# A hybrid decoder block with a product-key expert layer: expert-row fetches tied to TensorE's progress, and a second buffer in a lookup

## The chip, the cores and the metric

The kernel runs on one core of one Trainium2 chip. The metric is device time in microseconds of one execution, lower is better. Three timed executions of the kernel before are known, and one execution that was also profiled. Engines are called as the profile calls them: PE is TensorE (PEld its weight loads), DVE is VectorE, ACT is ScalarE, POOL is GpSimd, SP is SyncE, which here only issues DMAs.

## What is computed

One decoder layer over 512 tokens of width 1024: adaLN modulation, an input projection, sliding-window attention beside a short convolution, an output projection, and then an expert layer (PEER) over 16384 single-neuron experts. Only the expert layer matters for the change. Cut to it, the reference is:

```
q = (xt @ wq).reshape(T, 8 heads, 2, 128)
sc = einsum('thpd,hpkd->thpk', q, subkeys)          # 128 keys per half
vals, ids = top_k(sc, 16)
cand = vals[:, :, 0, :, None] + vals[:, :, 1, None, :]
top, pos = top_k(cand, 16)                          # 16 experts per head, 128 per token
idx = take(ids0 * 128 + ids1, pos); g = softmax(top)
a   = u_tab[idx] . x                                # one number per token and expert
out = sum over experts of g * gelu(a) * v_tab[idx]
x  += gate2 * out
```

## The kernel before

The 512 tokens are treated in two ways. For the first 384 (three chunks of 128) the expert layer is computed **densely**: all 16384 experts are taken as 128 groups of 128, and for each group j TensorE multiplies the tokens by the u table (the "u product" of j, line 197 to 199, called from `first`) and the gated result by the v table (the "v product" of j, line 958 to 960, called from `second`); a token's unused experts have a gate of zero. For the last 128 tokens the 128 chosen experts per token are **gathered**: `fetch` (line 764) has POOL issue an indirect DMA that brings, for expert number k of each of the 128 tokens, one row of 1024 numbers into a tile of 128 x 1024 (512 KB). There are 128 such fetches from the u table, each followed by a dot product on DVE (`dot`, line 774), then 128 from the v table, each followed by a multiply-and-add on DVE into the tile `ga` (line 872). Another 64 u fetches, earlier, serve the last 64 of the dense tokens (`last_dense`).

A u or v product takes three matmuls per block, since each operand is split into a high and a low part: a 512 KB table tile `raw` is loaded by SP (line 178, five buffers), ACT writes its high part `hi` (line 173), DVE the low part `lo` (line 174). A u product is 24 matmuls of 320 columns, a v product 18 matmuls of 512 columns.

The program, by stages in time, ends with two that the change touches:

- The **lookup** of the dense tokens (`lookup`, six steps of three chunks and two halves). Each step expands a table of key numbers on ACT into the tile `ex` (line 665), compares on DVE, multiplies the comparison by `ex` (line 686) and sums. Four u products are called between two steps (`LOOK`), so ACT's copies `sp<-pa` and `hi` stand between the expansions in ACT's queue. `ex` has one buffer for the three-chunk lookup (line 661).
- The **dense stage** (line 1005 on): a loop over j, 0 to 127. It calls the v product of j; from j = 64 on it also calls the u product of j + 8 (`first`), so u products end with j = 119. Each j needs its v tile (and its u tile), and every eighth j loads a block `G` of the gates (1536 KB); before j = 64 each pair of j also loads 320 KB `sp`. Beside each v product the loop runs a number of steps of `gathered()`, the generator that does the fetches: `PACE` (line 45) is the allowance per j, 1.75 before j = 64 and 4.2 from there on, and a fetch with its arithmetic takes 1.3 of it.

A fetch takes its tile in turn from two pools, `row` (six buffers, shared with `ga`) and `row2` (four buffers; the profile and the order write both as `row`). What stands in the queues is settled at build time: a scheduler goes over the whole program, orders the instructions of each engine by its own estimates and by which buffers are free, and adds the semaphore waits. On the chip each engine, POOL and SP too, runs its queue strictly in that order, so an instruction that waits holds all behind it.

Of the kernel before, what the change touches and what calls it, by code (L numbers as in the profile page):

```python
# [9 lines left out]
F16 = mybir.dt.float16  # L10
# [8 lines left out]
P = 128  # L19
# [11 lines left out]
NJ = 128  # L31
# [10 lines left out]
LAST = 8  # L42
NR = 3
WHEN = (-1, 0, 2, 3)
PACE = (1.75, 4.2)

# [40 lines left out]
def body(tc, p):  # L89
    nc = tc.nc  # L90
# [18 lines left out]
    def bank(name):  # L109
        return psm.tile([P, 512], F32, tag="m", name=name)  # L110
# [55 lines left out]
    def after(ins, mark):  # L166

        if mark is not None:
            tc.add_manual_dep(ins.ins, mark.ins.name, mybir.DependencyInfo(
                mybir.DependencyClass.Sync, mybir.DependencyReason.DATA), reason="pace")  # L170
# [10 lines left out]
    def parts(src):  # L181

        raw = load(src)
        h = hl.tile([P, D], F32R, tag="h", bufs=4, name="hi")
        l = hl.tile([P, D], F32R, tag="l", bufs=4, name="lo")
        split(h, l, raw)
        return h, l

    def weights_of(src):

        h, l = parts(src.rearrange("p a b -> p (a b)"))
        return (lambda k: h[:, k * P:(k + 1) * P]), (lambda k: l[:, k * P:(k + 1) * P])

    def mm3(ps, w, rh, rl, ks=range(DC), k0=0, k1=DC - 1):
        wh, wl = w
        for k in ks:
            nc.tensor.matmul(ps, wh(k), rh(k), start=(k == k0), stop=False)  # L197
            nc.tensor.matmul(ps, wh(k), rl(k), start=False, stop=False)  # L198
            mark[0] = nc.tensor.matmul(ps, wl(k), rh(k), start=False, stop=(k == k1))  # L199
# [13 lines left out]
    def tmp(name):  # L213
        return tp.tile([P, T], F32, name=name, **T2)
# [65 lines left out]
    for m, k in enumerate(ORDER):  # L280
# [10 lines left out]
        f = tmp("f")  # L291
# [184 lines left out]
    for step in PLAN.split():  # L476
        n = [int(x) for x in step[1:]]
# [104 lines left out]
    for r, (dst, cs) in enumerate(((hN, slice(TU - HT, TD)), (h2N, slice(TD, T)))):  # L582
        pg = [bank("pg0"), bank("pg1")]
        for k in range(DC):
            b = mod[:, 24 + k:25 + k]
            f = fs[k]
# [19 lines left out]
    def first():  # L606
        j = lead[0]
        if j == NJ:
            return
        lead[0] += 1  # L610
        w = weights_of(p["uL"][j])
        ps = psa.tile([P, TU], F32, tag="a", name="pa")
        mm3(ps, w, lambda k: h2H[:, k, :], lambda k: h2L[:, k, :])
        m, i = divmod(j, 2)
        if i == 0:
            ring[m] = up.tile([P, 2, TU], F32, name="sp", bufs=3) if j < SPILL else \
                rg.tile([P, 2, TU], F32, name="ge", bufs=RING)
        nc.scalar.activation(ring[m][:, i], ps, AF.Gelu_apprx_tanh)  # L618
        if i and j < SPILL:
            nc.sync.dma_start(Ad[m], ring.pop(m))  # L620
# [30 lines left out]
    def lookup(n, R, hs=slice(0, 8)):  # L651

        pl, pos = R["pool"], R["pos"][:, :, hs]
        nh = hs.stop - hs.start

        def it(name, dt, tag):
            return pl.tile([P, n, nh, 16], dt, tag=f"{tag}{n}", name=name, bufs=1)

        def wide(name):
            return rt.tile([P, nh, 16, 16], F16, name=name, **R2) if n == 1 else \  # L660
                pl.tile([P, nh, 16, 16], F16, tag=f"{name}{n}", name=name, bufs=1)

        def expanded(c, q):
            x = wide("ex")
            nc.scalar.activation(x, R["I"][:, c, hs, q, :, None].to_broadcast([P, nh, 16, 16]), AF.Copy)
            return x

        p4, p2 = it("p4", U32, "da"), it("p2", U32, "db")
        nc.vector.tensor_single_scalar(p4, pos, 4, op=OP.logical_shift_right)
        nc.vector.tensor_single_scalar(p2, pos, 2, op=OP.logical_shift_right)  # L670
        a, b = it("ra", F16, "ra"), it("rb", F16, "rb")
        nc.vector.scalar_tensor_tensor(a, p2, -12.0, p4, op0=OP.add, op1=OP.max)
        l12, b1 = it("l12", U32, "da"), it("rb1", F32, "db")
        nc.vector.tensor_single_scalar(l12, pos, 12, op=OP.bitwise_and)
        nc.vector.scalar_tensor_tensor(b1, pos, 64.0, l12, op0=OP.is_lt, op1=OP.mult)
        l2 = it("l2", U32, "da")
        nc.vector.tensor_single_scalar(l2, pos, 3, op=OP.bitwise_and)
        nc.vector.tensor_add(b, b1, l2)
        sh = [P, nh, 16, 16]
        for c in reversed(range(n)):  # L680
            for q, r, dst in ((0, a, R["i"]), (1, b, R["j"])):
                x = expanded(c, q)
                eq = wide("eq")
                nc.vector.tensor_tensor(eq, iotaA[:, None, :, :].to_broadcast(sh),
                                        r[:, c, :, None, :].to_broadcast(sh), op=OP.is_equal)
                nc.vector.tensor_mul(eq, eq, x)
                w = 8
                while w > 1:
                    nc.vector.tensor_add(eq[:, :, 0:w, :], eq[:, :, 0:w, :], eq[:, :, w:2 * w, :])
                    w //= 2  # L690
                nc.vector.tensor_add(dst[:, c, hs], eq[:, :, 0, :], eq[:, :, 1, :])
                yield
# [52 lines left out]
    last = None  # L745
    for hp in range(16):
# [3 lines left out]
        last = now  # L750
    scores(15, *last)
    weights(ND, Rd)
    first()
    first()
    more = [False, []]

    def numbers(dst, R, c, ks=slice(0, P)):
# [6 lines left out]
    def fetch(tab, e):  # L764
        more[0] = bool(more[1]) and not more[0]
        t = more[1][0].tile([P, D], F32, name="row2", bufs=4) if more[0] else r4.tile([P, D], F32, name="row", **R4)
        nc.gpsimd.indirect_dma_start(out=t, out_offset=None, in_=tab,  # L767
                                     in_offset=bass.IndirectOffsetOnAxis(ap=e, axis=0))
        return t

    def dot(a, e, h):
        t = fetch(p["uR"], e)
        junk = rt.tile([P, D], BF16, name="junk", **R2)
        nc.vector.scalar_tensor_tensor(junk, t, 1.0, h, op0=OP.mult, op1=OP.mult, accum_out=a)  # L774
# [39 lines left out]
    for c in range(ND):  # L814
# [3 lines left out]
        cs = slice(c * P, (c + 1) * P)  # L818
# [7 lines left out]
        n = P if c < ND - 1 else P - HT  # L826
# [19 lines left out]
    def gathered():  # L846

        Rg = results(1, rg)
        ei = rg.tile([P, P], I32, name="eG")
        av = rg.tile([P, P], F32, name="av")  # L850
        yield from route(Rg, ei, range(0, 4))
        others = route(Rg, ei, range(4, 8))
        for k in range(P):
            dot(av[:, k:k + 1], ei[:, k:k + 1], h2N)
            yield 1.3
            if k < P // 2:
                yield next(others, 0.0)
            if k == P // 2 - 1:
                for _ in others:
                    yield 2.0  # L860
                weights(1, Rg)
                yield 1.0
        nc.scalar.activation(av, av, AF.Gelu_apprx_tanh)
        nc.vector.tensor_mul(av, av, Rg["g"].rearrange("p c a b -> p (c a b)"))
        ga = r4.tile([P, D], F32, name="ga", **R4)
        vR = p["vL"].rearrange("j i d -> (j i) d")
        for k in range(P):
            t = fetch(vR, ei[:, k:k + 1])
            if k == 0:
                nc.vector.tensor_scalar_mul(ga, t, av[:, 0:1])  # L870
            else:
                nc.vector.scalar_tensor_tensor(ga, t, av[:, k:k + 1], ga, op0=OP.mult, op1=OP.add)  # L872
            yield 1.3
        total[0] = ga
# [72 lines left out]
    def second(js, ws):  # L947

        ops = [(*w, *parts(p["vL"][j])) for j, w in zip(js, ws)]
        for c, hf in [(c, hf) for hf in range(2) for c in range(ND)] if len(js) == 1 else \  # L950
                [(c, hf) for c in range(ND) for hf in range(2)]:
            cs = slice(c * P, (c + 1) * P)
            hs = slice(hf * 512, hf * 512 + 512)
            for j, (wh, wl, vh, vl) in zip(js, ops):
                if j == 0:
                    acc[c, hf] = bank(f"o{c}{hf}")
                o = acc[c, hf]
                nc.tensor.matmul(o, wh[:, cs], vh[:, hs], start=(j == 0), stop=False)  # L958
                nc.tensor.matmul(o, wh[:, cs], vl[:, hs], start=False, stop=False)  # L959
                nc.tensor.matmul(o, wl[:, cs], vh[:, hs], start=False, stop=(j == NJ - 1))  # L960

    def load_x1(c):
        x1 = r4.tile([P, D], F32, name="x1", **R4)
# [41 lines left out]
    for j in range(0, NJ, 2):  # L1005
        ws = gated(j // 2)
        for i in range(2):
            if j >= SPILL:
                first()
            if j < NJ - 2:  # L1010
                second([j + i], ws[i:])
            todo += PACE[j >= SPILL]
            while todo > 0:
# [75 lines left out]
```

## Time and profile before

| | |
|---|---|
| timed executions | 1494.27, 1496.88, 1503.24 us (median 1496.88) |
| the profiled execution, its own time | 1503.74 us |
| its span, first to last instruction | 1502.0 us |
| mean granted TensorE clock, share of full speed | 0.981 |
| busy share of the span: PE, DVE, ACT, POOL | 95%, 85%, 41%, 32% |
| moved by DMA | 432.07 MB |

The profile gives for each engine its instructions with start, duration and what they waited for, and for DMA the bytes and the mean busy share of 16 DMA engines. PE's busy time is a union of pipelined matmuls, so that PE seems busy where it is not at its peak; how fast it really goes is read from the starts of its matmuls. "Share" of DMA can go a little over 1, since a packet that starts in a window is counted there in full.

### The profile page before, as it was taken

The page shows a single profiled execution, that of the slowest core. Times are in us where ns is not written, and L with a number is a line of the kernel's source. Part 1 is how long each engine was busy: PE and PEld are TensorE (multiplying, and loading weights), DVE is VectorE, ACT ScalarE, POOL GpSimd, SP SyncE. Part 2 cuts the span into 40 slices and gives each one's busy share as a digit, 9 for nine tenths or more (in the row PEclk, how much of TensorE's full clock was granted, in tenths as well). Part 3 has the DMA queues.
Part 4 walks back from the last instruction along what each step waited for, and adds up shares of the span by engine and source line. Part 5 has one row for each costly group of instructions (what it writes and reads, how often), then busy time and mean ns, then how long its engine had stood idle before and what let it go on. Part 6 is the DMA issues. An engine that isn't in the chain of part 4 may idle for free.

```text
span 1502.0 us, 21357 instructions
## 1 busy us (share of the span) xinstructions
PE 1424.6 (95%) x7696; PEld 1239.3 (83%) x7696; DVE 1269.5 (85%) x2330; ACT 616.5 (41%) x1029; POOL 478.4 (32%) x324
## 2 busy tenths in 40 slices
PE   6999998999978999999999989999989999999998
PEld 4777776888977999999888867778879888889986
DVE  7878886999897899968799989899989999996445
ACT  4534537334543444454434333333424334244341
POOL 0000000000144133300234756667667677750000
PEclk9999999999988999999999999999999999999999
DMA  8644544332698699967899999999999999996443
GB/s 286 222 165 144 182 156 143 96 94 83 214 321 322 243 368 368 376 243 267 321 402 363 406 402 405 390 402 377 380 402 369 403 387 405 401 390 213 141 126 126
DMA packets 138283, 432.07 MB, mean 288 GB/s; under 512 B 13121, under 2 KB 39873, under 8 KB 136641
## 3 DMA queue, kind: packets, MB, share of 16 engines
q1 hardware_dynamic: 92096, 262.92, 48.2%
q0 software_dynamic: 46080, 167.79, 29.4%
q8 instruction: 60, 0.98, 0.3%
q14 instruction: 47, 0.38, 0.1%
HBM read 390.78 MB, written 39.85 MB: 287 GB/s over the span
## 4 chain that ended last, share of the span: by engine, by line
DMA 16%; DVE 13%; PE 13%; issue 10%; POOL 1%; ACT 1%; DVEq 0%; POOLq 0%; ACTq 0%; SPq 0%
DMA raw<-in_vL 6%; DMA raw<-in_uL 5%; DVE ga L872 4%; DMA row<-in_uR,eG 3%; DVE lo L174 3%; DVE junk L774 3%; PE o L959 3%; PE o L960 2%; PE o L958 2%; PE pa L197 2%; PE pa L199 2%; PE pa L198 2%; DVE wwl L174 2%; POOL row L767 1%; DVE w L941 1%
## 5 line engine op out<-in xcount | busy, mean ns | idle before, releaser
L173 ACT ACTIVATE hi<-raw 128x1024 fp32r<-128x1024 f32 x298 | 312.8, 1056 | 435.1 <-PE pa L198 137.9
L174 DVE TENSOR_TENSOR lo<-raw,hi 128x1024 fp32r<-128x1024 f32 x298 | 363.6, 1222 | 116.3 <-ACT hi L173 113.8
L197 PE MATMUL pa<-h2H,hi 128*128 128x320 f32 x1024 | 322.5, 315 | 24.8 <-ACT sp L618 19.6
L199 PE MATMUL pa<-h2H,lo 128*128 128x320 f32 x1024 | 320.2, 313 | 1.1 <-DVE lo L174 1.1
L198 PE MATMUL pa<-h2L,hi 128*128 128x320 f32 x1024 | 320.2, 313 | 0.0
L960 PE MATMUL o<-hi,wwl 128*128 128x512 f32 x768 | 303.3, 395 | 7.0 <-DVE wwl L174 4.0
L959 PE MATMUL o<-lo,wwh 128*128 128x512 f32 x768 | 303.5, 395 | 5.7 <-DVE lo L174 4.8
L958 PE MATMUL o<-hi,wwh 128*128 128x512 f32 x768 | 302.9, 394 | 5.9 <-ACT hi L173 5.9
L767 POOL DMA_INDIRECT row<-in_uR,eG x128 | 201.0, 1570 | 218.1 <-DVE w L941 96.2
L767 POOL DMA_INDIRECT row<-in_uR,eH x64 | 80.2, 1253 | 559.9 <-DVE lo L174 400.0
L767 POOL DMA_INDIRECT row<-in_vL,eG x128 | 197.0, 1539 | 88.6 <-DVE ga L872 56.9
L197 PEld LDWEIGHTS pa<-h2H,hi 128*128 128x128 f32 x1024 | 195.8, 191 | 29.5 <-ACT sp L618 21.0
L198 PEld LDWEIGHTS pa<-h2L,hi 128*128 128x128 f32 x1024 | 195.5, 191 | 2.1
L199 PEld LDWEIGHTS pa<-h2H,lo 128*128 128x128 f32 x1024 | 195.3, 191 | 1.9 <-DVE lo L174 1.9
L960 PEld LDWEIGHTS o<-hi,wwl 128*128 128x128 f32 x768 | 145.7, 190 | 44.7 <-DVE wwl L174 11.3
L959 PEld LDWEIGHTS o<-lo,wwh 128*128 128x128 f32 x768 | 145.5, 189 | 39.2 <-DVE lo L174 9.1
L958 PEld LDWEIGHTS o<-hi,wwh 128*128 128x128 f32 x768 | 145.7, 190 | 35.5 <-ACT hi L173 7.0
L872 DVE SCALAR_TENSOR_TENSOR ga<-row,av,ga 128x1024 f32<-128x1024 f32 x127 | 163.9, 1290 | 2.8 <-DMA row<-in_vL,eG 0.5
L774 DVE SCALAR_TENSOR_TENSOR junk<-row,h2N 128x1024 bf16<-128x1024 f32 x128 | 152.8, 1222 | 8.2 <-DMA row<-in_uR,eG 7.6
L940 ACT ACTIVATE w<-G 128x64 f32<-128x64 f32 x128 | 25.8, 248 | 240.0 <-DVE wwl L174 228.0
L916 PE MATMUL gps<-B,A 128*128 128x128 f16 x384 | 90.9, 297 | 1.9 <-DVE B L908 1.9
L774 DVE SCALAR_TENSOR_TENSOR junk<-row,hN 128x1024 bf16<-128x1024 f32 x64 | 78.1, 1221 | 15.2 <-DMA row<-in_uR,eH 15.2
(263 smaller groups left out, 1939.4 us busy)
## 6 DMA issues: line engine op xcount, KB each, us to landing
raw<-in_uL SPq DMA_DIRECT2D x128, 512.0 KB
raw<-in_vL SPq DMA_DIRECT2D x128, 512.0 KB
Gd<-st SPq DMA_DIRECT2D x12, 2048.0 KB
G<-Gd SPq DMA_DIRECT2D x16, 1536.0 KB
ada<-in_ada SPq DMA_DIRECT2D x32, 512.0 KB
Ad<-sp SPq DMA_DIRECT2D x32, 320.0 KB
sp<-Ad SPq DMA_DIRECT2D x32, 320.0 KB
raw<-in_w_in SPq DMA_DIRECT2D x18, 512.0 KB
```

Of the source, the lines that this page charges most:

```text
L173: nc.scalar.activation(h, f, AF.Copy)
L174: nc.vector.tensor_sub(l, f, h.bitcast(F32))
L197: nc.tensor.matmul(ps, wh(k), rh(k), start=(k == k0), stop=False)
L198: nc.tensor.matmul(ps, wh(k), rl(k), start=False, stop=False)
L199: mark[0] = nc.tensor.matmul(ps, wl(k), rh(k), start=False, stop=(k == k1))
L767: nc.gpsimd.indirect_dma_start(out=t, out_offset=None, in_=tab, in_offset=bass.IndirectOffsetOnAxis(ap=e, axis=0))
L774: nc.vector.scalar_tensor_tensor(junk, t, 1.0, h, op0=OP.mult, op1=OP.mult, accum_out=a)
L872: nc.vector.scalar_tensor_tensor(ga, t, av[:, k:k + 1], ga, op0=OP.mult, op1=OP.add)
L916: nc.tensor.matmul(o, A[:, b, :, t], B1[:, b, :, t], start=True, stop=False)
L958: nc.tensor.matmul(o, wh[:, cs], vh[:, hs], start=(j == 0), stop=False)
L959: nc.tensor.matmul(o, wh[:, cs], vl[:, hs], start=False, stop=False)
L960: nc.tensor.matmul(o, wl[:, cs], vh[:, hs], start=False, stop=(j == NJ - 1))
```

## The change

Three edits. `PACE` goes from 1.75 and 4.2 to 1.85 and 4.4. The three-chunk lookup gets two buffers for `ex`. And `fetch` ties its DMA to a v product: each call of `second` puts the last matmul of its v product on a list that keeps two; the next fetch, if two are there, takes the older one off and waits for it. So the first fetch that is called after the v product of j waits until TensorE has ended that of j - 1, and the fetches called after it, up to the next v product, wait for nothing new.

```diff
-PACE = (1.75, 4.2)
+PACE = (1.85, 4.4)
...
-                pl.tile([P, nh, 16, 16], F16, tag=f"{name}{n}", name=name, bufs=1)
+                pl.tile([P, nh, 16, 16], F16, tag=f"{name}{n}", name=name, bufs=2 if name == "ex" else 1)
...
+    done = []
     more = [False, []]
...
-        nc.gpsimd.indirect_dma_start(out=t, out_offset=None, in_=tab,
-                                     in_offset=bass.IndirectOffsetOnAxis(ap=e, axis=0))
+        d = nc.gpsimd.indirect_dma_start(out=t, out_offset=None, in_=tab,
+                                         in_offset=bass.IndirectOffsetOnAxis(ap=e, axis=0))
+        if len(done) > 1:
+            after(d, done.pop(0))
         return t
...
-                nc.tensor.matmul(o, wl[:, cs], vh[:, hs], start=False, stop=(j == NJ - 1))
+                last = nc.tensor.matmul(o, wl[:, cs], vh[:, hs], start=False, stop=(j == NJ - 1))
+        done.append(last)
+        del done[:-2]
```

`after(ins, mark)` adds a dependency: `ins` waits for `mark`. No instruction is added or taken away on PE, DVE or ACT, and PE's order is the same. DVE, POOL, ACT and SP get another order, since the scheduler knows of the new waits.

**POOL, dense stage, about the u rows 105 to 115 of the 128, before and then after.** `row_10469` and the like are tiles of the pool `row2`, plain `row` of the other; `in_uR` is the u table by rows, `eG` the expert numbers; `DMASW` are earlier fetches, `DVE` the release of a buffer, `PE` the new wait.

```order
L767 DMA row_10469<-in_uR,eG 128x1024 [waits DMASW0_49,DVE_49]
L767 DMA row<-in_uR,eG 128x1024 [waits DMASW1_49,DVE_49]
L767 DMA row_10542<-in_uR,eG 128x1024 [waits DMASW2_49,DVE_49]
L767 DMA row<-in_uR,eG 128x1024 [waits DMASW3_49,DVE_49]
L767 DMA row_10550<-in_uR,eG 128x1024 [waits DMASW4_49,DVE_49]
L767 DMA row<-in_uR,eG 128x1024 [waits DMASW5_49,DVE_49]
```

```order
L768 DMA row_10421<-in_uR,eG 128x1024 [waits DMASW1_49,DVE_49,PE_49]
L768 DMA row_10429<-in_uR,eG 128x1024 [waits DMASW2_49,DVE_49]
L768 DMA row_10493<-in_uR,eG 128x1024 [waits DMASW3_49,DVE_49]
L768 DMA row_10501<-in_uR,eG 128x1024 [waits DMASW4_49,DVE_49]
L768 DMA row_10574<-in_uR,eG 128x1024 [waits DMASW5_49,DMASW1_49,DVE_49]
L768 DMA row<-in_uR,eG 128x1024 [waits DMASW6_49,PE_49]
L768 DMA row<-in_uR,eG 128x1024 [waits DMASW7_49]
L768 DMA row<-in_uR,eG 128x1024 [waits DMASW0_49,PE_49]
L768 DMA row<-in_uR,eG 128x1024
```

Before, a fetch waited only for its buffer and an earlier fetch. Now about one in three or four also waits for PE, and those behind it in the queue wait with it. The PE wait of `row_10421` is for the v product of j = 73, the next two for 74 and 75.

**DVE, the end of the gathering, before and then after.** `lo<-raw,hi` is one table tile's low part (u or v), `ga<-row` uses one fetched v row, `w` and `wwl` prepare the gates of two j.

```order
L872 SCALAR_TENSOR_TENSOR ga<-row,av,ga 128x1024
L174 TENSOR_TENSOR lo<-raw,hi 128x1024
L941 TENSOR_TENSOR w<-ge,G 128x2x320
L872 SCALAR_TENSOR_TENSOR ga<-row_13710,av,ga 128x1024
L872 SCALAR_TENSOR_TENSOR ga<-row,av,ga 128x1024
L174 TENSOR_TENSOR lo<-raw,hi 128x1024
L872 SCALAR_TENSOR_TENSOR ga<-row_13716,av,ga 128x1024
L872 SCALAR_TENSOR_TENSOR ga<-row,av,ga 128x1024
L174 TENSOR_TENSOR lo<-raw,hi 128x1024
L174 TENSOR_TENSOR wwl<-w,wwh 128x768
L174 TENSOR_TENSOR lo<-raw,hi 128x1024
```

```order
L875 SCALAR_TENSOR_TENSOR ga<-row_13493,av,ga 128x1024
L875 SCALAR_TENSOR_TENSOR ga<-row,av,ga 128x1024
L174 TENSOR_TENSOR wwl<-w,wwh 128x768
L875 SCALAR_TENSOR_TENSOR ga<-row_13499,av,ga 128x1024
L174 TENSOR_TENSOR lo<-raw,hi 128x1024
L875 SCALAR_TENSOR_TENSOR ga<-row,av,ga 128x1024
L174 TENSOR_TENSOR lo<-raw,hi 128x1024
L875 SCALAR_TENSOR_TENSOR ga<-row_13570,av,ga 128x1024
L153 TENSOR_TENSOR dg<-cst,mod 128x1024
L875 SCALAR_TENSOR_TENSOR ga<-row,av,ga 128x1024
L174 TENSOR_TENSOR lo<-raw,hi 128x1024
```

Before, the last row is used behind the v tile of j = 106 and 34 more `lo` follow it. Now it is used behind the v tile of j = 120 and 7 follow. Counted over DVE's whole order, the rows used from behind the `lo` of one stage's first v tile to that of the next are, for j = 0 to 22, 23 to 63, 64 to 104, 105 to 118 and 119 on: 23, 79, 149, 5, 0 before; 12, 55, 138, 48, 3 after.

**ACT, the start of the lookup, the difference.** `ex` is the expansion, `sp<-pa` the copy of a u product out of PSUM, `hi` a table tile's high part, `Rg` a softmax.

```order
 L665 ACTIVATE ex<-I_2116 128x2048
 L618 ACTIVATE sp<-pa 128x320
-L173 ACTIVATE hi<-raw 128x1024 x2
-L618 ACTIVATE sp<-pa 128x320
-L173 ACTIVATE hi<-raw 128x1024
+L173 ACTIVATE hi<-raw 128x1024
+L665 ACTIVATE ex<-I_2116 128x2048
+L618 ACTIVATE sp<-pa 128x320
+L173 ACTIVATE hi<-raw 128x1024 x2
 L699 ACT_TABLE_LOAD
 L699 ACTIVATE Rg_2114<-Rg_2114 128x384
```

The second `ex` has moved up. From there on each `ex` stands where the one before it stood: the third at the old second's place, and the sixth at the old fifth's, while the old sixth's place is empty. DVE's order in the lookup is the same but for one `lo` that stands two rows later.

## Rows read from the trace of the kernel before

**Rows 1.** Page, DMA in 40 equal slices of 37.55 us: busy tenths, GB/s

```profile
DMA  8644544332698699967899999999999999996443
GB/s 286 222 165 144 182 156 143 96 94 83 214 321 322 243 368 368 376 243 267 321 402 363 406 402 405 390 402 377 380 402 369 403 387 405 401 390 213 141 126 126
```

**Rows 2.** Windows, dense stage in five: length, engines busy (x), clock, DMA share, GB/s

```profile
core 0: us, PE busy (x) PEld busy (x) DVE busy (x) ACT busy (x) POOL busy (x), PEclk, DMA share, GB/s
...
730.95:831.09 100.14, 96.69 (x417) 78.53 (x415) 92.66 (x216) 39.60 (x62) 46.30 (x34) 0.98 0.99 372
831.09:1022.49 191.40, 180.70 (x763) 143.67 (x761) 169.02 (x242) 62.39 (x101) 128.57 (x79) 0.97 1.03 401
1022.49:1351.87 329.38, 318.59 (x1723) 283.70 (x1723) 310.72 (x301) 122.11 (x189) 223.15 (x144) 0.99 1.01 390
1351.87:1458.55 106.68, 106.68 (x591) 96.53 (x589) 56.54 (x52) 43.26 (x66) 0.00 (x0) 1.00 0.50 159
1458.55:1502.00 43.45, 38.64 (x168) 30.98 (x166) 21.45 (x26) 10.27 (x14) 0.00 (x0) 1.00 0.37 133
```

**Rows 3.** Windows of line 958 alone, six matmuls per v product: PE, PEld (x)

```profile
730.95:831.09 100.14, 54.37 (x139) 26.35 (x139) 0.98 0.99 372
831.09:1022.49 191.40, 97.95 (x246) 47.09 (x245) 0.97 1.03 401
1022.49:1351.87 329.38, 96.32 (x247) 46.31 (x247) 0.99 1.01 390
```

**Rows 4.** Timeline of PE, 757.9 to 762.5 us: line 958, seventh start after the first

```profile
758.26 0.39 PE L958 MATMUL o<-hi,wwh 128*128 128x512 f32 x1
...
762.34 0.39 PE L958 MATMUL o<-hi,wwh 128*128 128x512 f32 x1
```

**Rows 5.** Timeline of PE, 1367 to 1375 us: two v products' first matmuls

```profile
1367.11 0.39 PE L958 MATMUL o<-hi,wwh 128*128 128x512 f32 x1
...
1374.73 0.39 PE L958 MATMUL o<-hi,wwh 128*128 128x512 f32 x1
```

**Rows 6.** Waits in 831.09:1022.49 and in 1022.49:1351.87: us, times, longest

```profile
ACT hi L173 <- DMA raw<-in_vL: 54.1, 15, 12.5
...
ACT hi L173 <- DMA raw<-in_uL: 48.5, 10, 13.4
```

**Rows 7.** The chain that ended last, in order of time: start, us, what

```profile
848.37 26.09 DMA raw<-in_vL
...
1044.28 9.76 DMA row<-in_uR,eG
...
1055.23 13.96 DMA row<-in_uR,eG
```

**Rows 8.** Windows of line 767 alone, the fetches: POOL busy (x)

```profile
730.95:831.09 100.14, 46.30 (x34) 0.98 0.99 372
831.09:1022.49 191.40, 128.57 (x79) 0.97 1.03 401
1022.49:1351.87 329.38, 223.15 (x144) 0.99 1.01 390
```

**Rows 9.** Timelines of POOL and DVE, 400 to 420 us: first fetch, its use

```profile
400.43 1.18 POOL L767 DMA_INDIRECT row<-in_uR,eH  x1 [399.98 <-DVE lo L174]
...
408.85 1.23 DVE L774 SCALAR_TENSOR_TENSOR junk<-row,hN 128x1024 bf16<-128x1024 f32 x1 [5.12 <-DMA row<-in_uR,eH]
```

**Rows 10.** Timeline, 417.2 to 421 us: lookup's fourth multiply, fifth expansion, PE

```profile
417.25 1.21 DVE L686 TENSOR_TENSOR eq<-eq,ex 128x2048 f16<-128x2048 f16 x1
...
418.56 1.91 ACT L665 ACTIVATE ex<-I 128x2048 f16<-128x2048 uint32 x1 [11.56 <-DVE eq L686]
...
420.85 0.64 PE L197 MATMUL pa<-h2H,hi 128*128 128x320 f32 x1 [8.08 <-ACT sp L618]
```

**Rows 11.** Windows, 10 us of the lookup: columns as in rows 2

```profile
415.00:425.00 10.00, 4.15 (x15) 4.15 (x16) 9.74 (x15) 4.46 (x5) 4.49 (x3) 0.59 0.84 287
```

**Rows 12.** Page, costliest groups, whole span: xcount, busy us, mean ns

```profile
L174 DVE TENSOR_TENSOR lo<-raw,hi 128x1024 fp32r<-128x1024 f32 x298 | 363.6, 1222 | 116.3 <-ACT hi L173 113.8
...
L872 DVE SCALAR_TENSOR_TENSOR ga<-row,av,ga 128x1024 f32<-128x1024 f32 x127 | 163.9, 1290 | 2.8 <-DMA row<-in_vL,eG 0.5
```

## Prediction

> **What bounds the kernel now.** I read the page's DMA slices first [rows 1]. From slice 20 to slice 35 (751 to 1352 us) DMA moves 363 to 406 GB/s, the highest in the run, and in the last four slices 126 to 213. So the dense stage has two halves: one in which the transfers are at their limit, and a tail in which they are idle by half.
>
> The windows by stage say what PE makes of it. I cut them at the starts of the v products of j = 23, 64, 105 and 119 [rows 2]; the matmuls of line 958, six per v product, give 139/6, 246/6 and 247/6, that is 23, 41 and 41 products, which leaves 14 and 9 [rows 3]. PE's own pace: the seventh start of line 958 is one product later than the first, 762.34 - 758.26 = 4.08 us for a v product alone [rows 4]; with a u product beside it, 1374.73 - 1367.11 = 7.62 us [rows 5]. The u products stand between the v products of j = 63 and 119, one in each gap. At that pace the stages would take 23 x 4.08 = 93.8, 40 x 4.08 + 7.62 = 170.8, 41 x 7.62 = 312.4 and 14 x 7.62 = 106.7 us. They took 100.1, 191.4, 329.4 and 106.7 [rows 2]. Lost: 6.3, 20.6, 17.0 and 0, together 43.9 us. The last stage (43.45 us) has 9 x 4.08 = 36.7 and the final evictions and stores, which stay.
>
> Who loses it for PE: in the second and third stage ACT's `hi` waits 54.1 us in 15 waits for v tiles and 48.5 us in 10 for u tiles [rows 6], and one of these loads is 26.09 us long on the chain [rows 7], while DMA has a share of 1.03 and 1.01 [rows 2]. The table tiles queue among the row fetches: POOL fetched 34, 79 and 144 rows in the first three stages and none after [rows 8] (256 in all; one is counted on both sides of a cut). So the fetches run too early for TensorE's good, and what they hurry towards is a tail of 23 products without any.
>
> **The change, part by part.** The sum is made against the profiled execution's own time, 1503.74 us. It is 6.9 us above the median of the three timed ones, 1496.88.
>
> *The wait for PE and the new order.* No work is added or removed; fetches move later. By the order of after, the fetches that stand ahead of the v products' waits fall to the stages as about 14, 57, 139 and 46 (before 34, 79, 143, 0). One row is 128 x 1024 x 4 bytes = 0.524 MB. The bytes of each stage are its rate by its length [rows 2]:
> - first stage 372 x 100.1 = 37.2 MB, less 20 rows (10.5) = 26.7 MB; at PE's pace (93.8 us) 285 GB/s, far below the limit;
> - second 401 x 191.4 = 76.8, less 22 rows (11.5) = 65.2 MB; in 170.8 us 382 GB/s;
> - third 390 x 329.4 = 128.5, less 4 rows (2.1) = 126.4 MB; in 312.4 us 405 GB/s;
> - fourth 159 x 106.7 = 17.0, plus 46 rows (24.1) = 41.1 MB; in 106.7 us 385 GB/s.
> What the transfers can carry is seen in the whole stages, 390 and 401 GB/s [rows 2], and in single slices, up to 406 [rows 1]. The second and fourth stage come under it; the third sits on it: 126.4 MB take 324.1 us at 390 and 315.2 at 401, so it loses between 11.7 and 2.8. I take 9, nearer to the stage's own rate. For the second I take 3 and for the fourth 2, since at 95% of the limit a tile is still late now and then (the bounds: 0, and at 378 GB/s 1.7 and 2.0). For the first I take 2: there one product waited for the first fetched rows, and the first fetch still comes when it came. Together 16 us are still lost, 43.9 - 16 = 28 us gained.
>
> *DVE.* In the third stage it was busy 310.7 us for 149 rows [rows 2]; 11 rows fewer at 1.29 [rows 12] make 296.5 of 312.4, or 7.23 us per j at 3.4 rows per j. The fourth gets the same mix, 48 rows for 14 j: about 102 of 106.7. So DVE fits, with 4 to 5% to spare, and its tail is no longer half idle.
>
> *What waits behind the new wait.* POOL's queue: the next rows. DVE's queue: a row's dot product or `ga`, and behind it the `lo` that PE needs next. That is a loop, and it holds as long as a row comes soon enough. Let T be the time from the end of the v product that is waited for to the start of the row's use on DVE. In the second stage a row gated by product j stands behind the `lo` of j + 4, so PE has four products, 16.3 us, and DVE at most two rows and a `lo` to do after it (2 x 1.29 + 1.22 = 3.8, [rows 12]): T may be 12.5. In the third stage up to about j = 82 PE has 2 x 7.62 = 15.2 us and DVE three or four rows and a `lo`, 5.1 or 6.4: T may be 10.1 or 8.8. From there on one row and a `lo`, 2.5: T may be 12.7. The trace has no gated fetch. The nearest row is the first fetch of all, 408.85 - 400.43 = 8.4 us from its start to its use, with DMA busy [rows 9]. The other end is the longest row piece of the chain, 13.96 us [rows 7], which is a late one by selection, in a queue that nothing held back. I take 9: it fits but for some 0.2 us in half of the j up to 82, which the 9 us contain.
>
> A rule of the Trainium skill speaks against the edit: "DMA: Bandwidth & Descriptors", Rules for kernel authors, has a DMA issued early and waited for late, so that its fixed cost hides behind compute. By that rule alone the fetches should not be held back, and the time would go the way of the slow rival below. The trace sides with it only where DMA has room: at a share of 1.03 the early issue is what makes the tiles late [rows 2, 6]. The same page, Anatomy of one DMA, puts a DMA from POOL at 2.0 us plus its bytes at 436 GB/s, which would be an estimate of 3.2 us for a row and leave the loop slack everywhere; the 8.4 us of the row are what I use.
>
> *PACE.* The larger allowance only calls the fetches earlier in the program; what holds them is the wait and the buffers, and the counts above are of the order that came out of both. Nothing apart.
>
> *Two buffers for `ex`.* In the lookup the fifth expansion waits 11.56 us for the fourth multiply, which DVE reaches at 417.25 behind dot products; ACT's `sp` copies stand behind it and PE waits 8.08 us [rows 10], and in the window around that idle time its granted clock is 0.59 on average, so for the most part the lower of its two levels, 1.2 GHz [rows 11]. With two buffers the n-th expansion waits for multiply n - 2. But each now stands where the one before it stood, so the sixth stands at the old fifth's place and waits for the fourth multiply as the fifth did: the same wait, with the same work behind it. I take 0. The bounds: -10 (the 8.08 us and a few at the low clock come back) and +2 (the second expansion, 1.91 us, now stands ahead of two `hi`).
>
> Sum: 1503.74 - 28 = 1475.7 by the profiled execution; by the median 1468.9. The timed runs scatter by 9 us and the profiled one is at their upper end, so I lean to the median: 1470.
>
> **The rivals.**
> *The transfers stay the limit.* If the mix of scattered rows and tiles carries no more than the two weakest slices in the middle, 377 and 380 GB/s [rows 1], the stages take 172.5, 334.4 and 108.7 us: 25.7 lost, with 5 for the first and for waits 31, a gain of 13, and about 1487. For it: slices below 390 do occur. Against: they are slices in which PE lacked nothing for long.
> *All waits go.* 43.9 us gained, 1453 by the median, 1460 by the profiled run, say 1455. For it: three of four stages have room. Against: the third has none.
> *The loop closes* (the slow one). Rows come after T = 14 us, as in the longest piece [rows 7]. Then PE loses (14 - 12.5)/4 in 41 products of the second stage, (14 - 9.5)/2 in some 19 of the third and (14 - 12.7)/2 in the 36 left: 15 + 43 + 23 = 81, with 4 besides 85, against 43.9: 41 slower, about 1538. It turns at T near 13, where as much is lost as before. For it: POOL's queue is strictly in order, and each gated fetch holds two or three more. Against: 8.4 us, and the gate itself keeps the queue short. The Trainium skill's rule above ("DMA: Bandwidth & Descriptors", Rules for kernel authors) would have it so.
> *The lookup gains.* Up to 10 us more, 1460. Against it is the order.
>
> **How the numbers follow.** Forecast 0.63, all waits gone 0.14, transfers 0.14, loop 0.06, lookup 0.03. About 1%, 15 us, is what a measurement of this kernel can tell from no change: faster means under 1482. The forecast, all gone and the lookup lie there (0.80) and a little of the transfers' case (0.03), together 0.83; the rest of it, and a loop that nearly breaks even, is 0.12; slower 0.05. The range reaches from below the case without waits by the median, 1450, to the transfers' case and a little above it, 1490; the loop is left out.
>
> **What would show it.** In the profile after: DMA near 400 GB/s through the third stage and 370 or more through the fourth, not 159; fetches until the v product of j = 117 has ended; ACT's waits for `raw` under a third of the 102.6 us; stage lengths about 96, 174, 321 and 109; ACT's expansion in the lookup still waiting 11 us. Wrong would be: the fourth stage without fetches; DVE waiting for rows by tens of microseconds (the loop); the third stage at 330 or more (the transfers); or an expansion that waits for nothing.

## The result, and the profile after

The changed kernel takes 1514.28 us (1513.13 to 1514.96), the kernel before beside it 1496.89: a ratio of 1.0106, with a 95% interval of 1.0078 to 1.0134. It is 1.1% slower, where 1470, 1.8% faster, was forecast. The profiled execution has a span of 1512.6 us, 10.6 more than before.

Where they went is seen in the windows of the changed kernel, cut at the same v products as [rows 2] (columns as there):

```profile
728.96:825.95 96.99, 95.30 (x416) 77.31 (x415) 81.85 (x192) 39.60 (x65) 15.40 (x14) 1.00 0.89 310
825.95:998.05 172.10, 171.18 (x763) 141.87 (x762) 148.62 (x203) 66.35 (x106) 79.41 (x59) 1.00 1.00 375
998.05:1347.89 349.84, 324.54 (x1725) 289.53 (x1724) 289.00 (x320) 120.54 (x187) 197.29 (x140) 0.98 0.96 352
1347.89:1464.99 117.10, 110.11 (x591) 96.25 (x589) 99.06 (x87) 37.62 (x58) 59.46 (x45) 1.00 0.96 352
1464.99:1512.60 47.61, 40.53 (x168) 32.11 (x166) 31.45 (x36) 12.66 (x19) 0.00 (x0) 0.96 0.38 134
```

The forecast lengths were 96, 174, 321 and 109 us. The first two stages came out so, 97.0 and 172.1, and gained 3.2 and 19.3. The third took 349.8, which is 20.5 more than before and 29 more than forecast; the fourth lost 10.4 and the last 4.2. With 2.0 gained ahead of the dense stage that is 20.5 + 10.4 + 4.2 - 3.2 - 19.3 - 2.0 = 10.6 us. A fuller DMA does not explain it: it moved 352 GB/s at a share of 0.96 in the third stage, where it had moved 390 at 1.01 [rows 2]. The page shows the same in its slices of 37.8 us, which answer to [rows 1]: the tail is filled, but no slice after the middle holds 400.

```profile
DMA  8544544322797799967898999999989899999974
GB/s 291 207 161 152 182 155 143 99 90 89 235 333 275 299 362 371 370 243 256 297 342 293 378 383 396 371 372 375 360 321 372 302 381 352 350 347 385 322 262 153
```

Who waits is on the page too. Ahead of the two groups of DVE that use rows, DVE now stands idle for 51.2 and 61.5 us, 50.0 and 54.7 of it for rows. Before, it was 2.8 [rows 12] and 8.2 in all. The two groups after, and then the second of them before:

```profile
L875 DVE SCALAR_TENSOR_TENSOR ga<-row,av,ga 128x1024 f32<-128x1024 f32 x127 | 163.0, 1283 | 51.2 <-DMA row<-in_vL,eG 50.0
L777 DVE SCALAR_TENSOR_TENSOR junk<-row,h2N 128x1024 bf16<-128x1024 f32 x128 | 152.5, 1224 | 61.5 <-DMA row<-in_uR,eG 54.7
```

```profile
L774 DVE SCALAR_TENSOR_TENSOR junk<-row,h2N 128x1024 bf16<-128x1024 f32 x128 | 152.8, 1222 | 8.2 <-DMA row<-in_uR,eG 7.6
```

And the waits in the third stage (engine, line, waited for: us, times, longest) say what POOL does meanwhile:

```profile
POOL row L768 <- DVE ga L875: 53.4, 23, 4.2
POOL row L768 <- PE o L963: 48.0, 19, 6.0
...
DVE ga L875 <- DMA row<-in_vL,eG: 31.6, 8, 6.0
...
PE pa L199 <- DVE lo L174: 19.1, 10, 3.3
POOL row L768 <- DVE junk L777: 17.9, 9, 4.5
ACT hi L173 <- DMA raw<-in_vL: 17.8, 4, 6.6
...
ACT hi L173 <- DMA raw<-in_uL: 3.1, 3, 1.3
```

DVE waits for rows, POOL waits for DVE, and PE waits for DVE's `lo`. POOL's waits for DVE are not new, and their sum alone does not show the cause. In the third stage before they were as long:

```profile
POOL row L767 <- DVE ga L872: 56.9, 58, 6.4
...
POOL row L767 <- DVE junk L774: 18.8, 9, 4.8
```

There a row was fetched long before its use (17.9 us from fetch to use, the median of the fetches from 1131 to 1352 us), so these waits held nobody up. What is new is which fetch stands behind them. The waits for table tiles have shrunk, as the change meant: 17.8 and 3.1 us here, against 48.5 for u tiles alone in that stage before [rows 6].

One place shows the loop. POOL's fetches in the changed kernel (start, duration, what ended the idle time ahead):

```profile
1171.26 1.68 POOL L768 DMA_INDIRECT row<-in_vL,eG  x1 [6.41 <-DMA row<-in_vL,eG]
1174.91 1.41 POOL L768 DMA_INDIRECT row<-in_vL,eG  x1 [1.97 <-DVE ga L875]
1179.30 1.68 POOL L768 DMA_INDIRECT row<-in_vL,eG  x1 [2.98 <-DVE ga L875]
1181.29 1.63 POOL L768 DMA_INDIRECT row<-in_vL,eG  x1 [0.30 <-issue]
```

These are, in the built order of POOL (numbers grow in the order of call, which is the order of use on DVE):

```
L768 DMA row2_11225<-in_vL,eG_6769 128x1024 [waits DMASW5_49,DMASW1_49,DVE_49]
L768 DMA row2_11231<-in_vL,eG_6769 128x1024 [waits DMASW6_49,DMASW2_49,DVE_49]
L768 DMA row2_11302<-in_vL,eG_6769 128x1024 [waits DMASW7_49,DMASW3_49,DVE_49]
L768 DMA row_11222<-in_vL,eG_6769 128x1024 [waits DMASW0_49,PE_49]
```

`row_11222` is needed first and stands last. Its gate, the v product of j = 84, ended at 1170.01 (the last matmul, in PE's timeline):

```profile
1169.62 0.39 PE L963 MATMUL o<-hi,wwl 128*128 128x512 f32 x1
```

but the three later rows ahead of it wait for DVE to give back their buffers, so that it starts 11.3 us after its gate opened. (For the first of the three the timeline names a landing. By the built order it also waits for the use of eight rows earlier, which ended at 1170.99, 0.27 us before the fetch started.) DVE then runs dry and waits for it (DVE's timeline):

```profile
1182.01 1.28 DVE L875 SCALAR_TENSOR_TENSOR ga<-row,av,ga 128x1024 f32<-128x1024 f32 x1
1183.21 1.22 DVE L174 TENSOR_TENSOR lo<-raw,hi 128x1024 fp32r<-128x1024 f32 x1
1188.56 1.28 DVE L875 SCALAR_TENSOR_TENSOR ga<-row,av,ga 128x1024 f32<-128x1024 f32 x1 [4.12 <-DMA row<-in_vL,eG]
1189.76 1.22 DVE L174 TENSOR_TENSOR lo<-raw,hi 128x1024 fp32r<-128x1024 f32 x1
```

So T, from the gate to the use, is 18.5 us here, against the 9 that was taken.

### The profile page after: what moved, and what is told of

Read it like the earlier page. It is cut to its first block, busy times and chain, and to the rows that moved or that the text cites. A ratio compares the mean times of both kernels' runs of the same rounds, so it can differ in the third digit from the quotient of the medians.

```text
span 1512.6 us, 21319 instructions
## 1 busy us (share of the span) xinstructions
PE 1425.6 (94%) x7696; PEld 1242.5 (82%) x7696; DVE 1268.3 (84%) x2330; ACT 615.7 (41%) x1029; POOL 433.1 (29%) x324
## 4 chain that ended last, share of the span: by engine, by line
PE 15%; DMA 12%; issue 12%; DVE 9%; POOL 6%; POOLq 0%; DVEq 0%; ACT 0%; SPq 0%
DMA row<-in_vL,eG 6%; POOL row L768 6%; DMA row<-in_uR,eG 5%; PE o L962 4%; PE o L963 4%; PE o L961 4%; DVE ga L875 2%; DVE lo L174 2%; DVE junk L777 1%; DVE wwl L174 1%; DMA G<-Gd 1%; DMA Gd<-st 1%; PE pa L197 0%; PE pa L199 0%; PE pa L198 0%
## 5 line engine op out<-in xcount | busy, mean ns | idle before, releaser
L768 POOL DMA_INDIRECT row<-in_uR,eG x128 | 178.0, 1391 | 316.8 <-PE o L963 171.7
L199 PEld LDWEIGHTS pa<-h2H,lo 128*128 128x128 f32 x1024 | 196.4, 192 | 25.7 <-DVE lo L174 25.7
L768 POOL DMA_INDIRECT row<-in_vL,eG x128 | 173.6, 1356 | 150.0 <-DVE ga L875 89.3
L875 DVE SCALAR_TENSOR_TENSOR ga<-row,av,ga 128x1024 f32<-128x1024 f32 x127 | 163.0, 1283 | 51.2 <-DMA row<-in_vL,eG 50.0
L777 DVE SCALAR_TENSOR_TENSOR junk<-row,h2N 128x1024 bf16<-128x1024 f32 x128 | 152.5, 1224 | 61.5 <-DMA row<-in_uR,eG 54.7
L943 ACT ACTIVATE w<-G 128x64 f32<-128x64 f32 x128 | 25.9, 249 | 346.3 <-DVE wwl L174 327.8
```

The costliest lines, as they stand in the source:

```text
L768: d = nc.gpsimd.indirect_dma_start(out=t, out_offset=None, in_=tab, in_offset=bass.IndirectOffsetOnAxis(ap=e, axis=0))
```

## The experiments

Two theories were set against each other. Q: the order of POOL's queue, later rows ahead of the gated one. G: the gate itself, too late however the queue is ordered. Stage lengths of all kernels, in us, from windows cut as above (one profiled execution each):

| kernel | median | to j = 23 | to 64 | to 105 | to 119 | to the end |
|---|---|---|---|---|---|---|
| before | 1496.89 | 100.1 | 191.4 | 329.4 | 106.7 | 43.4 |
| changed | 1514.28 | 97.0 | 172.1 | 349.8 | 117.1 | 47.6 |
| e1 fetches in order | 1468.56 | 95.7 | 170.8 | 320.7 | 106.7 | 43.8 |
| e2 older gate | 1512.97 | 97.0 | 175.5 | 353.2 | 117.3 | 44.0 |
| e3 gates to j = 64 | 1487.10 | 97.0 | 172.1 | 331.5 | 112.7 | 43.4 |
| e4 no gate | 1498.81 | 103.7 | 187.1 | 325.5 | 106.7 | 43.4 |
| e5 every fetch gated | 1467.37 | 96.1 | 170.8 | 315.1 | 107.4 | 44.2 |
| e6 before, in order | 1500.28 | 99.4 | 196.4 | 327.4 | 106.7 | 43.4 |
| e7 gates and order alone | 1465.19 | 96.4 | 170.8 | 313.3 | 106.7 | 45.9 |
| e8 in order, 2.3 and 3.9 | 1471.33 | 95.7 | 182.6 | 312.4 | 106.7 | 43.5 |
| e9 gates alone | 1491.04 | 95.4 | 171.6 | 330.4 | 113.2 | 48.4 |
| e10 in order, 2.0 and 4.2 | 1462.72 | 95.8 | 171.7 | 315.0 | 106.7 | 43.7 |
| e11 one ahead at most | 1468.46 | 96.2 | 171.4 | 318.5 | 112.6 | 43.8 |
| e12 two ahead at most | 1472.57 | 95.5 | 172.3 | 325.9 | 107.8 | 43.4 |

**e1, the queue in order.**

```diff
         if len(done) > 1:
             after(d, done.pop(0))
+        if last:
+            tc.add_manual_dep(d.ins, last[0].ins.name, mybir.DependencyInfo(
+                mybir.DependencyClass.NoSync, mybir.DependencyReason.SCHED_ONLY), reason="order")
+        last[:] = [d]
         return t
```

> Edit: the changed kernel, and each fetch is kept behind the fetch called before it in POOL's queue (an edge for the order alone, no wait on the chip). Gates as in the changed kernel. Theory Q (queue order): the loop closes because up to three fetches of later rows, each waiting for DVE to give back a buffer, stand in POOL's queue ahead of the gated fetch whose row is needed first. Then the third stage (v products j = 64 to 104) falls from 349.8 us to 320 to 328, the fourth from 117.1 to 107 to 110, and the time to about 1480 (1475 to 1490). Theory G (the gate itself): from the end of v product j to the use behind the v tile of j + 2 there is too little time however POOL is ordered. Then the third stage stays at 343 or more and the time at 1505 to 1516.

Measured: 1468.56 us, ratio to before 0.9793 (0.9752 to 0.9834), with the same gates and the same number of rows in each stage. Its windows:

```profile
997.12:1317.85 320.73, 315.96 (x1725) 283.66 (x1723) 292.91 (x323) 120.34 (x187) 199.34 (x140) 0.99 1.00 384
1317.85:1424.53 106.68, 106.68 (x591) 96.52 (x589) 103.43 (x92) 40.98 (x63) 59.52 (x45) 1.00 1.00 389
```

and POOL's waits in its third stage:

```profile
POOL row L769 <- PE o L968: 89.0, 36, 8.2
POOL row L769 <- issue: 31.8, 101, 1.3
```

POOL now waits for PE more, 89.0 against 48.0 us, and for row buffers not at all, and the stage is 29 us shorter. The time is below the 1475 to 1490 that was expected. The gate did not cost the time, and this speaks for Q. But e1 alone does not tell POOL's order from DVE's: compared by operation and tile, 38 of DVE's 1805 instructions and 6 of ACT's 1000 stand elsewhere than in the changed kernel (PE's and SP's order is the same). e12, below, tells them apart.

**e2, an older gate.** `len(done) > 2`, `del done[:-3]`.

> Edit: the changed kernel with a list of three v products instead of two, so that each gated fetch waits for the product one earlier: 7.6 us more from gate to use where u products run, 4.1 us before. Queue order still with later rows ahead. Theory G: the third stage falls to 320 to 328 us, the time to about 1480 (1474 to 1490). Theory Q: the fetches that stand ahead wait for DVE, not for PE, so little changes: third stage above 338, time 1500 to 1514.

Measured: 1512.97, ratio 1.0096 (1.0062 to 1.0129). The number fits Q, but the experiment does not speak against G, because its premise failed: in the built order each use moved forward by one product together with its gate (the fetch gated by j = 72 is used behind the v tile of 74, as that of 73 had been behind 75), so nothing had more time: in both kernels every gated row from j = 64 on is used two v tiles behind its gate.

**e3, gates only before j = 64.** The list is emptied after each v product of j = 64 or more.

> Edit: the changed kernel with gates only before j = 64 (the list is emptied from there on). Both theories: the first two stages stay at about 97 and 172 us as in the changed kernel, the third and fourth go back to about 329 (325 to 335) and 107 to 110, time about 1482 (1476 to 1490): faster than before and after. If instead the allowance or the second lookup buffer costs something, it stays above 1495.

Measured: 1487.10, ratio 0.9906 (0.9869 to 0.9943). The gain of the first two stages stays, the third is back at 331.5 (329.4 before), and the fourth, which now has rows, takes 112.7, 6 more than before, where 107 to 110 was expected. It is the part of the change that works as built.

**e4, no gate.** The two lines with `after(d, ...)` left out.

> Edit: the changed kernel without any gate: the new allowance and the second lookup buffer alone. If the gates are the whole of it, the time is that of the kernel before, 1491 to 1500, with rows spread 23, 79, 149, 5, 0 over the stages as before. If the allowance costs time by itself, it is above 1502; if the second buffer gains in the lookup, below 1490.

Measured: 1498.81, ratio 1.0010 (0.9985 to 1.0035): without gates, allowance and second buffer do nothing together.

**e5, every fetch gated.** `after(d, done[0])` in place of `done.pop(0)`.

> Edit: the changed kernel, but the product waited for stays on the list, so that every fetch waits for it and not only the first one after a v product. More waits, none of them later than before; no edge between fetches. As a side effect no fetch can be put ahead of its gate, and POOL's queue comes out with at most one later row ahead of an earlier one. Theory Q (queue order): the same as with the order fixed, third stage 318 to 326 us, time 1463 to 1475. Theory G (waits for PE cost the time): more waits, so no better than the changed kernel, 1505 or more.

Measured: 1467.37, ratio 0.9789 (0.9742 to 0.9835). The built program carries 108 waits for PE, as many as the changed kernel, since behind a gated fetch its group need not wait again. With every row tied to its product it takes 47 us less: theory G is out. In the built order no more than one fetch has a later row ahead of it. The third stage, 315.1 us, is below the 318 to 326 that was expected.

**e6, the kernel before in order.** The edge of e1 on the kernel before.

> Edit: the kernel before, no gates, with the edge that keeps each fetch behind the fetch called before it. Theory Q: later rows stand ahead of earlier ones in the kernel before too, but there a row is asked for some 15 to 20 us before its use, so that order costs nothing and mending it gains nothing: 1490 to 1502, DMA near 400 GB/s in the second stage and idle by half after 1352 us. If the order alone is what made the first run of the experiments fast, without the gates, this one falls to 1475 or less.

Measured: 1500.28, ratio 1.0006 (0.9979 to 1.0033). The order alone gains nothing; it counts only with gates.

**e7, gates and order alone.** e1 with `PACE = (1.75, 4.2)` and `bufs=1`.

> Edit: the kernel before with the gates and with the order edge, but the old allowance (1.75 and 4.2) and one buffer for the key numbers. By the built order 16 rows are then used behind the v tiles of j = 119 on, against 3. If the allowance counts only together with the gates: the tail, where v products alone run at 4.1 us and DVE has a row and a lo for each, takes 5 to 15 us more, time 1473 to 1485. If the allowance is worth nothing here either: 1464 to 1472.

Measured: 1465.19, ratio 0.9772 (0.9726 to 0.9818). The second outcome: the longer tail (45.9 against 43.8) is more than paid by the third stage, 313.3 with 134 fetches against 320.7 with 140. What gains is gates and order.

**e8, more rows early.** e1 with `PACE = (2.3, 3.9)`.

> Edit: the first run of the experiments (gates, order fixed) with an allowance of 2.3 and 3.9 instead of 1.85 and 4.4, which moves 15 rows from the third stage and 6 from the fourth to the first two (15, 74, 123, 42, 2). The third stage there is at the limit of the transfers (320.7 us against 312.4 at TensorE's pace, 384 GB/s); 15 rows are 7.9 MB, 20 us of transfer at 390 GB/s. If transfers hold it: third stage 312 to 316, second 171 to 174, time 1458 to 1466. If something else holds it (the rows' own loop): third stage 319 to 323, time 1466 to 1472.

Measured: 1471.33, ratio 0.9806 (0.9759 to 0.9853). The third stage runs at TensorE's pace exactly, as was expected if transfers held it. (Fewer rows also ease DVE's loop. And e5 brings 139 rows there in 315.1 us, at 390 GB/s, so not all of e1's 8 us above that pace belong to the number of rows.) But the second stage now does what the third did:

```profile
827.30:1009.94 182.64, 173.72 (x763) 141.43 (x762) 166.45 (x232) 64.76 (x105) 106.93 (x75) 1.00 1.03 398
1009.94:1322.36 312.42, 312.42 (x1724) 282.68 (x1723) 279.54 (x289) 121.64 (x188) 161.18 (x123) 1.00 1.00 373
```

75 fetches need 398 GB/s there, and 11.8 of the 182.6 us are lost. The forecast time, 1458 to 1466, was missed by that.

**e9, gates alone.** e7 without the edge.

> Edit: the kernel before with the gates alone: old allowance, one buffer for the key numbers, no order edge. Theory Q: it is slow like the changed kernel, 1500 to 1518, since later rows stand ahead of gated ones here too (0.55 of them on average against 0.73); third and fourth stage together 440 us or more, against 420.0 with the order edge on the same kernel. If the new allowance is what hurt together with the gates, it is faster than 1485.

Measured: 1491.04, ratio 0.9965 (0.9947 to 0.9983). The expected time was missed on both sides. Third and fourth stage are 330.4 + 113.2 = 443.6 us, against 420.0 with the edge, as Q had it; but the first two gain, so that it is 0.4% faster than before.

```profile
992.74:1323.15 330.41, 318.32 (x1725) 286.20 (x1723) 281.15 (x318) 120.77 (x187) 188.08 (x134) 0.98 0.97 364
1323.15:1436.30 113.15, 109.12 (x591) 97.60 (x590) 99.72 (x88) 40.51 (x63) 60.61 (x45) 0.98 0.95 355
```

The edge is worth 1491.04 - 1465.19 = 25.9 us here and 1514.28 - 1468.56 = 45.7 with the new allowance (by the ratios 1.9% and 3.1%). So the allowance (with the second buffer) does cost time, 23 us, but only by way of the queue.

**e10, between.** e7 with `PACE = (2.0, 4.2)`.

> Edit: the kernel before with gates, order edge and an allowance of 2.0 and 4.2, between the two tried; rows by the built order 13, 61, 133, 45, 4. The second stage held TensorE's pace with 59 rows and lost 12 us with 74; the third lost 0.9 us with 131 and nothing with 123. If rows per stage are what decides: second stage 171 to 174, third 313 to 317, the tail 43.4 to 44.5 instead of 45.9, time 1458 to 1465. If not, 1465 to 1472, as the others in order.

Measured: 1462.72, ratio 0.9773 (0.9749 to 0.9797), the lowest median of all, though by its ratio no better than e7 (0.9772). The stages came out as expected.

```profile
822.19:993.91 171.72, 171.28 (x764) 141.87 (x762) 155.49 (x214) 66.17 (x105) 91.34 (x65) 1.00 1.02 391
993.91:1308.92 315.01, 313.18 (x1724) 282.55 (x1723) 288.15 (x311) 120.22 (x187) 187.71 (x133) 1.00 1.01 384
```

**e11 and e12, how many may stand ahead.** The edge leads to the third, then the fifth fetch before instead of the last one (`last[-3]`, `last[-5]`). The built orders, for the rows used from j = 63 on, have so many fetches with one, two, three later rows ahead: before 58, 15, 1; changed 36, 22, 20; e9 47, 12, 12; e1 none; e11 57, 0, 0; e12 56, 22, 0.

> Edit: the changed kernel with a looser order edge, each fetch behind the third one before it. By the built order at most one later row then stands ahead of an earlier one (57 fetches from j = 63 on have one, none has more). Theory B (the wait for a buffer): the fetch for use n + 1 waits until DVE has done use n - 7; at 3.4 rows per 7.62 us that is 7 rows or 15.7 us ahead of use n, more than the 11 to 12 us that two fetches on POOL, a row's way (8.2) and its use take. So nothing is lost against the full order: 1463 to 1475. Rival P (each later row ahead costs POOL's time, whatever it waits for): 57 of the 140 rows ahead that the changed kernel has, so 57/140 of its 45.7 us: about 1487 (1482 to 1492).

> Edit: the same with each fetch behind the fifth one before it: at most two later rows ahead (56 fetches with one, 22 with two, none with three). Theory B: the second one waits for use n - 5, 5 rows or 11.2 us ahead of use n, about what is needed, so little is lost: 1467 to 1488; it is the third, at 3 rows or 6.7 us, that closes the loop. Rival P: 100 of 140, about 1501 (1495 to 1507).

Measured: 1468.46, ratio 0.9788 (0.9753 to 0.9822), and 1472.57, ratio 0.9813 (0.9777 to 0.9849). Against e1, at most one ahead costs nothing by the median (though in e11's profiled execution the fourth stage takes 112.6 us), two some 4 us (inside the intervals), three 45.7 us. That is the step that theory B (the wait for a buffer) draws, and not the 19 and 33 us of a cost for each row ahead (rival P). It also settles what e1 left open: in e12 6 of DVE's instructions stand elsewhere than in the changed kernel, and none of PE's, ACT's and SP's, but 20 of POOL's 330 do, and it is 41.7 us faster. In e12's third stage POOL's waits for buffers are down to a third, beside the 53.4 and 17.9 above:

```profile
POOL row L769 <- DVE ga L880: 16.0, 10, 2.9
POOL row L769 <- DVE junk L782: 5.0, 2, 4.4
```

## Why the prediction was wrong

**The bound and the gain were right.** Row fetches too early for TensorE, table tiles late behind them, an idle tail: with the queue in order, the same gates give 95.7, 170.8, 320.7 and 106.7 us for the forecast 96, 174, 321 and 109, and 1468.56 us for the forecast 1470. Third-stage DMA has a share of 1.00 there, at 384 GB/s, and the stage loses 8.3 us to TensorE's pace for the 9 of the sum; with fewer rows (e8) it loses nothing. That all of it is the transfers' limit is not shown, since e5 loses 2.7 us with one fetch fewer, at 390 GB/s.

**The step that failed is T**, "the time from the end of the v product that is waited for to the start of the row's use on DVE", and of it the sentence "I take 9". The 8.4 us of [rows 9] are the way of a row from the start of its fetch. Taking them for T supposes that the gated fetch starts when its gate opens. I paired each gated fetch of the changed kernel with the end of its product and with its use: the median of T is 8.45 us in the second stage (40 fetches), where the loop held and the stage came out as forecast; 11.3 from 998 to 1131 us, 13.1 from 1131 to 1348 and 13.6 in the fourth stage, where 9.5 and 12.7 were allowed. With the queue in order (e1) it is 8.9, 9.5, 10.2 and 9.5: there the 9 was a fair value. Most of the difference is time in POOL's queue. From 1131 us on T is, by the mean, 13.5 us in the changed kernel and 10.5 in e1, and 2.5 of these 3.0 us lie between the gate and the start of the fetch: the nine gated fetches with three later rows ahead start 6.2 us after their gate (median), the fifteen with one ahead 0.3 us, as in e1. The rest, behind the start, is probably DVE held up by the late rows before; no run parts it. Put into the formula of the slow rival, the mean T of the last three groups (11.3, 13.5 and 13.8 us for 16, 25 and 13 fetches) gives an estimate of 31 us lost, of the 39.5 by which the changed kernel's third and fourth stage are longer than e1's.

Why a fetch is held follows from the buffers. A fetch takes a tile in turn from two pools, so a later row in the pool `row2`, of four buffers, waits until DVE has done the use eight rows earlier. Standing ahead of the row for use n as the first, second or third such row, it holds that fetch until use n - 7, n - 5 or n - 3 is done: at 3.4 rows per 7.62 us that is 15.7, 11.2 or 6.7 us ahead of use n, while a use (1.3), a fetch ahead (1.7 + 0.3, as in the timeline) and a row's way (8.2, the median from start to use of the gated fetches in the second stage) take 11.5. By this estimate the loop closes on DVE itself with three ahead, whatever PE does, and e11 and e12 bear it out.

**It could have been seen.** The order of POOL quoted with the change has `row_10493`, `row_10501` and `row_10574` ahead of the first plain `row` that waits for PE. By DVE's order that row is used before all three, and two more of the plain ones before `row_10574`; printed without numbers, they hid that. The argument against the slow rival, "the gate itself keeps the queue short", looked at how much stood in the queue and not at which row stood first.

**The slow rival** was the right kind (rows late, DVE waiting for rows by tens of microseconds, the sign named for it), at 0.06 and with 1538 by a T of 14. It put the price on the wait for PE and the row's way. e5 and e1, with as many waits, show that this wait is not what costs. The Trainium skill's rule of issuing a DMA early and waiting late ("DMA: Bandwidth & Descriptors", Rules for kernel authors) agrees with the sign of the changed kernel; it differs from e1, which holds its fetches back by the same gates and is 2.1% faster than before.

**The rival of the transfers** rests on a misread row. It took 377 and 380 GB/s for the two weakest slices of the middle; between slices 20 and 35 [rows 1] has 363 and 369. Its sign, a third stage at 330 or more, came, but not by its cause: e1, with the same rows, has 320.7. The sum's 3 us for the second stage lies outside the bounds it names, 0 and 1.7; the changed kernel lost 1.3 there.

**PACE, "nothing apart"**, was wrong: e9 against the changed kernel, 23 us. The two differ in the second buffer too; without gates it has no visible part (e4), and with gates no run parts the two. By the built orders, the larger allowance brings 42 instead of 24 fetches with two or three later rows ahead. With the queue in order the difference is 3.4 us (e1 against e7), inside the intervals.

**Two buffers for `ex`, 0**, held within the scatter: the expansion still waits 8.71 us, where it waited 11.56 [rows 10] and 11 was forecast.

```profile
417.57 1.91 ACT L665 ACTIVATE ex<-I 128x2048 f16<-128x2048 uint32 x1 [8.71 <-DVE eq L686]
```

The dense stage starts 2.0 us earlier in the changed kernel, but over all profiled executions it starts at 723.5 to 732.4 us with two buffers and at 725.6 to 731.0 with one.

**DVE's room** held too: 103.4 us busy of 106.7 in e1's fourth stage, for a forecast of 102.

## What to carry to other kernels

When a wait is put on an instruction that a scheduler orders, look in the built order at what it now puts ahead of that instruction in the same queue, by the order of use, and at what those wait for: here the gates were worth 2% and their side effect on the order 3%. Tying the whole group to the same event (e5), or an edge for the order alone (e1), keeps the gain. What a fetch waits for is best counted in uses of its consumer: a buffer that comes free eight uses earlier is ample for its own row and can be too late for the one queued behind it, here when three such fetches stood ahead.

## What the runs showed of the hardware

A fetch on POOL lasts 0.94 us while DVE is idle, and 1.49 us on average and up to 2.43 while DVE works. POOL in the changed kernel:

```profile
1064.63 1.99 POOL L768 DMA_INDIRECT row<-in_uR,eG  x1 [0.30 <-issue]
1066.93 1.70 POOL L768 DMA_INDIRECT row<-in_uR,eG  x1 [0.30 <-issue]
1068.93 0.94 POOL L768 DMA_INDIRECT row<-in_uR,eG  x1 [0.30 <-issue]
1070.18 0.94 POOL L768 DMA_INDIRECT row<-in_uR,eG  x1 [0.30 <-issue]
```

DVE had nothing between 1068.55 and 1072.97:

```profile
1067.73 0.82 DVE L944 TENSOR_TENSOR w<-ge,G 128x640 f32<-128x640 f32 x1
1072.97 1.22 DVE L777 SCALAR_TENSOR_TENSOR junk<-row,h2N 128x1024 bf16<-128x1024 f32 x1 [4.42 <-DMA row<-in_uR,eG]
```

Pairing all 320 fetches with DVE's busy time: the 56 that fall into idle time (DVE busy for less than a fifth of them) last 0.94 us each (0.935 to 0.945), the 233 under a busy DVE (for 85% of them or more) 1.49 on average, though 35 of these are as short as the others; in the kernel before it is 25 with 0.94 and 267 with 1.57. At 3.4 rows per j and 0.3 of issue for each, fetches of 1.49 would take an estimated 6.1 of POOL's 7.62 us, and fetches of 2.0 all of it. No run was made on this alone, and why some fetches under a busy DVE are long and some not is open.
